# Four state-space scans joined into one stream over chunks of tokens, with GpSimd's arithmetic moved to VectorE

## Chip, core and metric

One NeuronCore of a Trainium2 chip runs the whole block as one program. TensorE (PE in the profile, its weight loads PEld) multiplies matrices, VectorE (DVE) and ScalarE (ACT) work element by element, GpSimd (POOL) too, and SyncE (SP) issues most of the transfers. The metric is the device time of one execution in microseconds; lower is better.

## The reference, cut to what matters

An encoder block on 1040 tokens (16 meta tokens and 1024 of the input) of width 1024: one wide projection, a convolution branch, a bidirectional Mamba-2 branch, a gated merge, and a mixture of 16 experts. The change touches the projections and the Mamba-2 branch.

```python
proj = jnp.einsum('btd,dk->btk', u, w_in[l])          # conf_a, conf_g, z, xbc, dt, gates
xbc = jax.nn.silu(depthwise_conv(xbc, w_ssm_conv[l], b_ssm_conv[l]))       # 7 taps
# xs: 32 heads of 64; Bs, Cs: 4 groups of 128 states
y = bidir_ssd(xs, dt_raw, ssm_dt_bias[l], ssm_a_log[l], Bs, Cs, ssm_d[l])
y = rms_norm(y * jax.nn.silu(z), w_ssm_norm[l])
branch_ssm = jnp.einsum('btc,cd->btd', y, w_ssm_out[l])

# ssd_scan, one direction, chunks of 128 tokens:
y_diag = jnp.einsum('bcgls,bcgjls,bcsgjp->bclgjp', cb, decay, xd)          # within a chunk
states = jnp.einsum('bclgn,bcgjl,bclgjp->bcgjpn', Bc, decay_to_end, xd)
# prev: carry * chunk_decay + states, from chunk to chunk
y_off = jnp.einsum('bclgn,bcgjpn,bcgjl->bclgjp', Cc, prev, jnp.exp(a_cs))  # from the state
# bidir_ssd: forward + backward + d_skip * xs
```

## The kernel before

The kernel is written in Tile: a scheduler lays out every engine's queue ahead of time from the program's order, from marked priorities (`tc.high_priority`) and from its own timeline; on the chip each queue then runs strictly in that order, and an instruction that waits holds all behind it.

The front of the program has two kinds of work. **Projections:** 73 blocks of 128 columns of `w_in`, each in three parts of some 347 tokens (a third). A third is 24 matmuls in fp16 (lines 97 to 99, three products of split operands) into a PSUM tile `mm`, of which there are three. `xbc_tile` (line 362) copies a third from PSUM on ACT and then runs the 7-tap convolution `po` on DVE (line 378); `do_conf` (line 313) makes `ci` and leaves 30 taps (line 335) in a list, from which `some_taps` (line 308) takes a few at a time; `ci` and `co` have one buffer. `gate_tile` (line 340) and `z_tile` (line 350) apply tanh; z's product on DVE (line 358) reads PSUM itself. Weights are converted by ACT (line 224) and DVE (line 225).

**Scans:** `group(g)` (line 531) runs the four groups one after the other. For each of 9 chunks, `within` (line 560) loads the rows of decay, makes them on ACT, multiplies by `cb` on DVE (line 584), and `add_within` (line 589) adds the result `py` to the sum `xs` of the whole group (line 600). `state` and `pass_state` (lines 602 and 617) carry the state forward and backward, two halves for each chunk: `yo` times `er` on DVE (line 628), the sum on GpSimd (line 630), the new state by GpSimd (line 639) and DVE (line 641). `scaled` (line 552) makes `xw` on GpSimd (line 556). The projections of the next group are spread between the halves by `fill`. `turn` (line 387) transposes `po` and stores it to `xk_d`; it is called 4 or 6 thirds after its tile.

A group begins with loads of `Bt`, `Ct` and `xs` for all tokens and ends with all taps that are left, the gating product (line 677) and the store of `yz_d`. GpSimd's queue also holds the stores to DRAM. After the fourth group, `y_group` (line 741) loads `yz_d` and `conf_norm` (line 708) loads `conf_d`, both on ACT's queue, and the next stage multiplies by `w_ssm_out`. The experts (from about 1720 us) are the larger part of the program.

## Time and profile before

| | us |
|---|---|
| median of 3 runs (3063.12 to 3075.85) | 3065.05 |
| the profiled execution | 3077.56 |
| its span, first to last instruction | 3075.9 |
| PE busy in it | 2772.1 (90%) |
| DVE busy | 2214.2 (72%) |
| ACT busy | 1683.7 (55%) |
| POOL busy | 827.2 (27%) |

The profiled execution has 1.7 us around its span and lies 12.5 us above the median. Times in the views are microseconds from the span's start. The program can be cut by its PE work: setup to 85, projections and scans to 1243 (the four groups' first scan products start at 233, 478, 756 and 1009), the branch outputs to 1720, the experts to the end.

### The profile page before, as it was taken

Reading aid. Unit: us, or ns where it says so; the run is one execution under the profiler, and the core shown is the slowest. Engines: PE = TensorE matmul, PEld = TensorE weight load, DVE = VectorE, ACT = ScalarE, POOL = GpSimd, SP = SyncE. Lnnn points to the kernel's source line nnn. Section 1 sums busy time; section 2 is a strip of 40 time slices with the busy share of each in tenths; the row PEclk is TensorE's granted clock in tenths of the full one; section 3 lists DMA queues with packets and bytes.
Section 4 is the critical chain, followed back from the end, with each engine's and each line's share of the span. In section 5 each row is a group of like instructions: output and inputs, shape, how many; then the busy total and the mean of one; then the engine's idle time right before and its main releaser. Section 6 shows DMA issues by size and latency. Waiting matters only on the chain. (4 is left out here: it accounts for less than half of the span.)

```text
span 3075.9 us, 64985 instructions
## 1 busy us (share of the span) xinstructions
PE 2772.1 (90%) x27584; PEld 2372.7 (77%) x27584; DVE 2214.2 (72%) x2747; ACT 1683.7 (55%) x2499; POOL 827.2 (27%) x714
## 2 busy tenths in 40 slices
PE   6789889898999889498999798999999999999996
PEld 4556556565656556498978698999999999999996
DVE  6857966995995798757646587777677777777673
ACT  6646565645665541244313376666666666666643
POOL 1115534542642462223000001112221222222213
PEclk8899999898999989799999899999999999999998
DMA  5345555547456551531533688999999999999994
GB/s 146 116 141 156 161 169 201 163 130 230 154 177 193 185 165 64 184 100 49 184 100 126 244 325 291 333 334 333 327 338 327 318 333 334 325 340 343 341 320 142
DMA packets 370675, 687.88 MB, mean 224 GB/s; under 512 B 31713, under 2 KB 139585, under 8 KB 370377
## 3 DMA queue, kind: packets, MB, share of 16 engines
q1 hardware_dynamic: 335376, 580.64, 55.4%
q0 software_dynamic: 24928, 71.69, 7.7%
q10 hardware_dynamic: 10080, 31.40, 3.3%
q8 instruction: 216, 3.54, 0.5%
q14 instruction: 75, 0.61, 0.1%
HBM read 608.64 MB, written 75.01 MB: 222 GB/s over the span
## 5 line engine op out<-in xcount | busy, mean ns | idle before, releaser
L97 PE MATMUL gu<-xT,wh 128*128 128x130 f16 x3968 | 698.9, 222 | 3.7 <-ACT sil L1134 3.7
L99 PE MATMUL gu<-xT,wl 128*128 128x130 f16 x3968 | 697.7, 220 | 1.2 <-DVE wl L1105 1.1
L98 PE MATMUL gu<-xT,wh 128*128 128x130 f16 x3968 | 698.8, 220 | 0.0
L1091 ACT ACTIVATE junk<-wst 128x2048 bf16<-128x2048 f32 x248 | 473.8, 1910 | 385.4 <-DMA wst<-in_w_exp_gate_dram 321.4
L1105 DVE SCALAR_TENSOR_TENSOR wl<-wst,sc,wh 128x2048 f16<-128x2048 f32 x248 | 572.6, 2346 | 26.9 <-ACT wh L1102 23.9
L98 PEld LDWEIGHTS <-wh 128*128 128x128 f16 x4856 | 480.9, 99 | 82.8 <-issue 38.2
L97 PEld LDWEIGHTS <-wh 128*128 128x128 f16 x4856 | 475.3, 98 | 51.7 <-issue 7.6
L99 PEld LDWEIGHTS <-wl 128*128 128x128 f16 x4832 | 471.3, 98 | 47.5 <-DVE wl L1105 1.5
L1157 PE MATMUL dn<-ac,wst 128*128 128x130 f32 x3840 | 459.3, 277 | 0.0
L1157 PEld LDWEIGHTS dn<-ac,wst 128*128 128x128 f32 x3840 | 440.7, 191 | 0.0
L1176 POOL DMA_INDIRECT h<-yo,idx x60 | 181.9, 3032 | 911.2 <-DVE yo L1175 758.3
L335 DVE SCALAR_TENSOR_TENSOR co<-ci,ct,co 128x1040 f32<-128x1040 f32 x240 | 356.0, 1484 | 3.8 <-ACT co L332 1.7
L97 PE MATMUL mm<-uh,wh 128*128 128x346 f16 (+3 forms) x888 | 280.6, 316 | 22.7 <-DVE st L358 11.2
L97 PE MATMUL mm<-uh,wl 128*128 128x346 f16 (+1 forms) x864 | 275.9, 319 | 17.6 <-DVE st L358 7.9
L98 PE MATMUL mm<-ul,wh 128*128 128x346 f16 (+3 forms) x888 | 280.2, 316 | 0.0
L99 PE MATMUL mm<-uh,wh 128*128 128x346 f16 (+3 forms) x888 | 279.3, 315 | 0.0
L98 PE MATMUL mm<-ul,wl 128*128 128x346 f16 (+1 forms) x864 | 275.3, 319 | 0.0
L99 PE MATMUL mm<-uh,wl 128*128 128x346 f16 (+1 forms) x864 | 275.3, 319 | 0.0
L1102 ACT ACTIVATE wh<-wst,sc 128x2048 f16<-128x2048 f32 x124 | 241.3, 1996 | 19.4 <-DVE sc L1068 17.9
L556 POOL TENSOR_TENSOR xw<-xk,dtw 128x512 f32<-128x512 f32 (+1 forms) x136 | 200.5, 1486 | 129.9 <-DMA xk<-xk_d 82.6
L581 ACT ACTIVATE row<-row,cst 128x128 f32<-128x128 f32 (+1 forms) x576 | 168.9, 378 | 108.0 <-DMA row<-cs_d 106.0
L378 DVE SCALAR_TENSOR_TENSOR po<-pre,sp,po 128x1040 f32<-128x1040 f32 x144 | 204.4, 1420 | 2.7 <-ACT po L375 1.6
(358 smaller groups left out, 4887.9 us busy)
## 6 DMA issues: line engine op xcount, KB each, us to landing
wst<-in_w_exp_gate_dram SPq DMA_DIRECT2D x128, 1024.0 KB, 8.1
wst<-in_w_exp_up_dram SPq DMA_DIRECT2D x128, 1024.0 KB, 9.5
wst<-in_w_exp_down_dram SPq DMA_DIRECT2D x128, 1024.0 KB, 7.9
wr<-in_w_in_dram SPq DMA_DIRECT2D x73, 512.0 KB, 5.3
row<-cs_d SPq DMA_DIRECT2D x64, 512.0 KB, 5.0
xk<-xk_d SPq DMA_DIRECT2D x92, 320.0 KB, 3.6
er<-ecs_d SPq DMA_DIRECT2D x120, 128.0 KB, 3.2
xk_d<-xt POOLq DMA_DIRECT2D x20, 512.0 KB, 4.7
```

What stands on the lines that cost most here:

```text
L97: pe.matmul(ps, wh(k), xh(k), start=(k == 0), stop=False)
L98: pe.matmul(ps, wh(k), xl(k), start=False, stop=False)
L99: pe.matmul(ps, wl(k), xh(k), start=False, stop=(k == K - 1))
L335: dve.scalar_tensor_tensor(co, ci[:, m:m + T], ct[:, m:m + 1], co, op0=OP.mult, op1=OP.add)
L378: dve.scalar_tensor_tensor(po, pre[:, m:m + T], sp[:, j, m:m + 1], po, op0=OP.mult, op1=OP.add)
L556: pool.tensor_mul(heads(o[:L]), heads(xk[:L, :512]), dtw[:L, c, w, hs].unsqueeze(2).to_broadcast([L, HG, 64]))
L581: act.activation(out=E[:L, j, :L], in_=E[:L, j, :L], func=AF.Relu, scale=-1.0, bias=cs)
L1091: act.activation(out=junk, in_=t[m][b], func=AF.Square, accum_out=sq[:, b, m:m + 1])
L1102: act.activation(out=wh[m][0], in_=t[m][0], func=AF.Copy, scale=sc[:, 1, m:m + 1])
L1105: dve.scalar_tensor_tensor(wl[m][b], t[m][b], sc[:, 1, m:m + 1], wh[m][b], op0=OP.mult, op1=OP.subtract)
L1157: pe.matmul(last["dn"][b // 3][:, b % 3], t[:, k, b * P:b * P + P], ac[:, 2 * i + k], start=(i + k == 0 and b % 3 == 0), stop=(i == 7 and ...
L1176: nc.gpsimd.indirect_dma_start(out=h2_d[b], in_=yo[:, h], in_offset=None, compute_op=OP.add, out_offset=bass.IndirectOffsetOnAxis(ap=r.idx ...
```

## The change

- The four groups' scans form one list of 36 chunks and 72 halves; chunks of the next group are prepared while the last ones of a group run. No group waits for its taps to end.
- The sum is kept by chunk: `xa` (ten buffers) is loaded from `xs_d` for one chunk, and `add_to` adds `py` and both directions' `er` on DVE. When a chunk's last term is in, its part of `sz_d` is loaded into a buffer of `er` (of which there are two), multiplied and stored to `yz_d`, which is now one DRAM tile for each group. `Bt` and `Ct` are replaced by chunk loads `bc_` and `Cc`.
- D is put in by ACT when `po` is stored; the gate's factor by ACT in `z_tile` (`zt`), whose product on DVE now reads no PSUM. z and gate are staged by thirds.
- `xw`, the new state's product and the sum go from GpSimd to DVE. GpSimd keeps the stores and the fills.
- `cb` gets a PSUM buffer of its own; `st` keeps one. `po` has three buffers; the convolution has a higher priority; `turn` comes 8 thirds after its tile. Projections are in another order, and the taps taken per half are 2, 4, 3, 5.

```diff
-    sz_d = dram.tile([16, P, T], F32, name="sz_d")
-    yz_d = dram.tile([16, P, T], F32, name="yz_d")
+    sz_d = [dram.tile([4, P, T], F32, name=f"sz_d{g}") for g in range(GR)]
+    yz_d = [dram.tile([4, P, T], F32, name=f"yz_d{g}") for g in range(GR)]
...
         def gate_tile(j):
             w = wtile(OFF_GATE + j * P)
-            st = stage.tile([P, T], F32, name="st")
             for t0, n in NCH:
                 ps = proj(w, t0, n)
+                st = stage.tile([P, 348], F32, name="st")
                 with soon():
-                    act.activation(out=st[:, t0:t0 + n], in_=ps, func=AF.Tanh, scale=w[3])
+                    act.activation(out=st[:, :n], in_=ps, func=AF.Tanh, scale=w[3])
+                nc.gpsimd.dma_start(gate_d[j, :, t0:t0 + n], st[:, :n])
                 yield
-            nc.gpsimd.dma_start(gate_d[j], st)
 
         def z_tile(j):
             w = wtile(OFF_Z + j * P)
-            pool.tensor_copy(zinv[:, j:j + 1], w[3])
-            st = stage.tile([P, T], F32, name="st")
             for t0, n in NCH:
                 ps = proj(w, t0, n)
+                st, zt = [stage.tile([P, 348], F32, name="st") for _ in range(2)]
                 with soon():
-                    act.activation(out=st[:, t0:t0 + n], in_=ps, func=AF.Tanh, scale=w[3])
-                    dve.scalar_tensor_tensor(st[:, t0:t0 + n], st[:, t0:t0 + n], 1.0, ps, op0=OP.add, op1=OP.mult)
+                    act.activation(out=st[:, :n], in_=ps, func=AF.Tanh, scale=w[3])
+                    act.activation(out=zt[:, :n], in_=ps, func=AF.Copy, scale=w[3])
+                dve.scalar_tensor_tensor(st[:, :n], st[:, :n], 1.0, zt[:, :n], op0=OP.add, op1=OP.mult)
+                nc.gpsimd.dma_start(sz_d[j // 4][j % 4, :, t0:t0 + n], st[:, :n])
                 yield
-            nc.gpsimd.dma_start(sz_d[j], st)
+            gated.append(j)
+
+        gated = []
...
-            po = b1.tile([P, T], F32, name="po", bufs=2)
+            po = b1.tile([P, T], F32, name="po", bufs=3)
             act.activation(out=po, in_=pre[:, 0:T], func=AF.Identity, scale=sp[:, j, 0:1], bias=sp[:, j, 7:8])
-            with tc.high_priority(offset=200):
+            with tc.high_priority(offset=900):
                 for m in range(1, TS):
                     dve.scalar_tensor_tensor(po, pre[:, m:m + T], sp[:, j, m:m + 1], po, op0=OP.mult, op1=OP.add)
                 act.activation(out=po, in_=po, func=AF.Silu)
-            nc.gpsimd.dma_start(xs_d[g][i] if i < 4 else bc_d[g][i - 4], po)
+                if i < 4:
+                    act.activation(out=pre[:, 0:T], in_=po, func=AF.Copy, scale=d2[:, 4 * g + i:4 * g + i + 1])
+            nc.gpsimd.dma_start(xs_d[g][i] if i < 4 else bc_d[g][:, i - 4], pre[:, 0:T] if i < 4 else po)
             if i < 5:
-                xt = b1.tile([P, NTT, P], F32, name="xt")
-                later.extend([(third[0] + (6 if g else 4), lambda c0=c0: turn(g, i, po, xt, c0)) for c0 in (0, 1, 5)])
+                later.extend([(third[0] + 8, lambda c0=c0: turn(g, i, po, c0)) for c0 in (0, 1, 5)])
...
+            xt = b1.tile([P, 4, P], F32, name="xt", bufs=2)
             with soon():
-                act.activation(out=xt[:L, c0:c0 + len(cs)], in_=ps[:L, :len(cs)], func=AF.Copy)
-            cols = slice(i * P, i * P + P)
-            if c0 == 0:
-                nc.gpsimd.dma_start(xk_d[g][0, :NMETA, cols], xt[:NMETA, 0])
-            elif c0 == 5:
-                nc.gpsimd.dma_start(xk_d[g][1:, :, cols].rearrange("c p n -> p c n"), xt[:, 1:])
+                act.activation(out=xt[:L, :len(cs)], in_=ps[:L, :len(cs)], func=AF.Copy)
+            nc.gpsimd.dma_start(xk_d[g][c0:c0 + len(cs), :L, i * P:i * P + P].rearrange("c p n -> p c n"),
+                                xt[:L, :len(cs)])
+            if c0 == 5:
+                turned_.add((g, i))
...
+        first = x_(0, 4) + c_(0) + x_(0, 5, 0) + g_(0) + x_(0, 1, 2) + g_(1) + x_(0, 3) + z_(0, 1, 2)
+        plan = [x_(1, 4) + z_(3) + x_(1, 5, 0) + c_(1) + x_(1, 1) + g_(2) + x_(1, 2, 3) + g_(3, 4) + z_(4, 5),
+                x_(2, 4) + z_(6) + c_(2) + z_(7) + x_(2, 5, 0, 1) + g_(5) + x_(2, 2, 3) + c_(3) + z_(8, 9),
+                x_(3, 4) + z_(10) + x_(3, 5) + z_(11) + c_(4) + x_(3, 0, 1) + g_(6) + x_(3, 2, 3) + g_(7, 8) + z_(12, 13),
+                z_(14, 15) + c_(5) + g_(9, 10) + c_(6) + g_(11, 12) + c_(7) + g_(13, 14, 15)]
...
+                def scaled(g, xk, c, w, d):
+                    L = TOK[c][1]
+                    hs = slice(32 * d + HG * g, 32 * d + HG * g + HG)
+                    o = s2.tile([P, 512], F32, name="xw", bufs=3)
+                    dve.tensor_mul(heads(o[:L]), heads(xk[:L, :512]),
+                                   dtw[:L, c, w, hs].unsqueeze(2).to_broadcast([L, HG, 64]))
+                    return o
+
+                sums = {}
+
+                def sum_of(g, c):
+                    t0, L = TOK[c]
+                    if (g, c) not in sums:
+                        xa = s2.tile([P, 4, P], F32, name="xa", bufs=10)
+                        nc.sync.dma_start(xa[:, :, :L], xs_d[g][:, :, t0:t0 + L].rearrange("i p t -> p i t"))
+                        sums[g, c] = [xa, 0]
+                    return sums[g, c]
+
+                def add_to(g, c, y):
+                    t0, L = TOK[c]
+                    s = sums[g, c]
+                    dve.tensor_add(s[0][:, :, :L], s[0][:, :, :L], y[:, :, :L])
+                    s[1] += 1
+                    if s[1] == (2 if c in (0, 8) else 3):
+                        assert all(4 * g + i in gated for i in range(4))
+                        sz = s2.tile([P, 4, P], F32, name="er")
+                        nc.sync.dma_start(sz[:, :, :L], sz_d[g][:, :, t0:t0 + L].rearrange("i p t -> p i t"))
+                        dve.tensor_mul(sz[:, :, :L], sz[:, :, :L], s[0][:, :, :L])
+                        nc.gpsimd.dma_start(yz_d[g][:, :, t0:t0 + L].rearrange("i p t -> p i t"), sz[:, :, :L])
...
+                    bc_ = s2.tile([P, 2, P], F32, name="bc_")
+                    nc.sync.dma_start(bc_[:, :, :L], bc_d[g][:, :, t0:t0 + L])
...
+                    sum_of(g, c)
+                    yield
+                    ps = sps.tile([P, P], F32, name="cb")
+                    pe.matmul(ps[:L, :L], bc_[:, 0, :L], bc_[:, 1, :L], start=True, stop=True)
+                    yield
...
+                    with tc.high_priority(offset=700):
+                        add_to(g, c, py)
...
+                    if c != (8 if d else 0):
+                        sum_of(g, c)
+                        Cc = s2.tile([P, P], F32, name="Cc")
+                        nc.sync.dma_start(Cc[:, :L], bc_d[g][:, 1, t0:t0 + L])
...
-                                    pool.tensor_mul(heads(Sn), heads(S),
-                                                    etot[:, c, hs].unsqueeze(2).to_broadcast([P, HG, 64]))
...
+                                dve.tensor_mul(heads(Sn), heads(S),
+                                               etot[:, c, hs].unsqueeze(2).to_broadcast([P, HG, 64]))
...
+                units = [(g, c) for g in range(GR) for c in range(NTT)]
+                halves = [(g, d, 8 - i if d else i) for g in range(GR) for i in range(NTT) for d in range(2)]
+                work = thirds([i for p_ in plan for i in p_])
...
-                        some_taps(4 if g in (1, 3) else 2)
...
-                    some_taps(TK)
-                    for i in range(4):
-                        sz = b1.tile([P, T + 6], F32, name="pre", bufs=2)[:, :T]
-                        nc.sync.dma_start(sz, sz_d[4 * g + i])
-                        dve.scalar_tensor_tensor(sz, sz, zinv[:, 4 * g + i:4 * g + i + 1], xs[:, i], op0=OP.mult,
-                                                 op1=OP.mult)
-                        nc.gpsimd.dma_start(yz_d[4 * g + i], sz)
...
+                    if m == per - 3:
+                        while later:
+                            later.pop(0)[1]()
+                    some_taps((2, 4, 3, 5)[g])
...
```

Where the instructions stand now, at three places. First DVE's queue in the middle of the third group's scan. `xs` and `xa` are sums, `S` the state, `po` and `co` the two convolutions. Before:

```order
L600 TENSOR_TENSOR xs<-xs,py 128x4x128
L335 SCALAR_TENSOR_TENSOR co<-ci,ct,co 128x1040
L584 TENSOR_TENSOR row<-row,cbm_7606 128x1024
L584 TENSOR_TENSOR row<-row,cbm_7608 128x1024
L628 TENSOR_TENSOR er<-yo,er 128x512
L641 TENSOR_TENSOR S_7695<-st,S_7695 128x512
L378 SCALAR_TENSOR_TENSOR po<-pre,sp,po 128x1040
```

Now:

```order
L562 TENSOR_TENSOR xa<-xa,py 128x512
L545 TENSOR_TENSOR xw<-xk,dtw 128x512
L207 TENSOR_SCALAR sc<-sc 128x3
L380 SCALAR_TENSOR_TENSOR po<-pre,sp,po 128x1040
L562 TENSOR_TENSOR xa<-xa,er 128x512
L648 TENSOR_TENSOR er<-yo,er 128x512
L658 TENSOR_TENSOR S_8231<-S_7989,etot 128x512
```

The products `xw` and `S` by `etot` and the sum `xa` by `er` stand between DVE's own work; before, they were on GpSimd's queue.

Second SP's queue, late in a group's scan (the last group before, the second now). `er` takes turns between two buffers. Before:

```order
L613 DMA er_10555<-ecs_d_74 64x512 x2
L549 DMA xk_10800<-xk_d3_72 128x640
L195 DMA wr_10467<-in_w_in_dram 128x8x128
L613 DMA er_10648<-ecs_d_74 64x512 x2
L613 DMA er_10804<-ecs_d_74 64x512 x2
```

Now:

```order
L629 DMA Cc_6777<-bc_d1_62 128x16
L578 DMA bc__7429<-bc_d2_63 128x2x128
L633 DMA er_6330<-ecs_d_80 64x512 x2
L567 DMA er_6409<-sz_d1_68 128x4x128
L633 DMA er_6458<-ecs_d_80 64x512
L567 DMA er_6578<-sz_d1_68 128x4x128
```

Every second buffer of `er` now holds a chunk of `sz_d`, and loads of the next group's chunks stand between them.

Third ACT's queue at the end of the front, where the last tanh (`st`) is followed by the next stage's loads. Before:

```order
L766 DMA gt<-gate_d 128x1040 x2
L346 ACTIVATE st<-mm,sc 128x346 x2
L160 ACTIVATE wh<-wr 128x512
L712 DMA cc<-conf_d 128x1040 x7
L748 DMA yst<-yz_d 128x1040 x2
L712 DMA cc<-conf_d 128x1040
L750 ACTIVATE yh<-yst,cp 128x1040 x2
```

Now:

```order
L345 ACTIVATE st<-mm,sc 128x346 x2
L160 ACTIVATE wh<-wr 128x512
L774 DMA yst<-yz_d_71 128x1040 x2
L776 ACTIVATE yh<-yst,cp 128x1040 x2
L778 ACTIVATE yst<-yst 128x1040 x2
L774 DMA yst<-yz_d_71 128x1040 x2
L776 ACTIVATE yh<-yst,cp 128x1040 x2
L778 ACTIVATE yst<-yst 128x1040
L738 DMA cc<-conf_d 128x1040
```

The loads of `yz_d` have gone ahead of those of `conf_d`.

## Rows read from the trace of the kernel before

**Rows 1.** Windows: each engine's busy time by stage of the front; then the totals.

```profile
core 0: us, PE busy (x) PEld busy (x) DVE busy (x) ACT busy (x) POOL busy (x), PEclk, DMA share, GB/s
85.00:233.00 148.00, 124.13 (x795) 81.53 (x795) 102.20 (x116) 79.10 (x152) 23.67 (x47) 0.92 0.43 132
233.00:478.00 245.00, 214.14 (x1525) 146.42 (x1524) 190.99 (x207) 142.83 (x285) 114.79 (x106) 0.95 0.54 172
478.00:756.00 278.00, 241.81 (x1675) 162.65 (x1673) 229.35 (x246) 151.27 (x296) 109.88 (x109) 0.93 0.56 175
756.00:1009.00 253.00, 228.81 (x1613) 154.63 (x1613) 190.18 (x213) 149.29 (x296) 115.36 (x111) 0.95 0.57 181
1009.00:1243.00 234.00, 212.32 (x1501) 145.00 (x1502) 207.80 (x215) 93.23 (x197) 107.61 (x80) 0.95 0.41 130
85.00:1243.00 1158.00, 1021.22 (x7102) 690.23 (x7103) 920.51 (x997) 615.72 (x1224) 471.31 (x450) 0.94 0.51 161
1243.00:1300.00 57.00, 19.26 (x93) 17.11 (x90) 35.60 (x26) 18.32 (x25) 15.82 (x11) 0.72 0.61 210
```

**Rows 2.** Waits of PE, 85 to 1243: total us, times, longest.

```profile
PE mm L392 <- ACT po L379: 34.5, 8, 12.5
PE mm L97 <- DVE st L358: 19.1, 12, 3.3
PE st L570 <- DVE S L641: 15.6, 8, 4.1
PE st L633 <- issue: 9.4, 4, 3.9
PE py L596 <- POOL xw L556: 7.8, 4, 2.7
```

**Rows 3.** Groups by form, 85 to 1243: count, busy us, mean ns, idle before.

```profile
L335 DVE SCALAR_TENSOR_TENSOR co<-ci,ct,co 128x1040 f32<-128x1040 f32 x237 | 352.1, 1486 | 3.8 <-ACT co L332 1.7
L378 DVE SCALAR_TENSOR_TENSOR po<-pre,sp,po 128x1040 f32<-128x1040 f32 x139 | 197.9, 1425 | 2.7 <-ACT po L375 1.6
L584 DVE TENSOR_TENSOR row<-row,cbm 128x1024 f32<-128x1024 f32 x64 | 106.8, 1696 | 4.7 <-ACT row L582 4.7
...
L556 POOL TENSOR_TENSOR xw<-xk,dtw 128x512 f32<-128x512 f32 x124 | 188.4, 1530 | 108.7 <-DMA xk<-xk_d 61.5 <-PE st L633 30.9 <-PE py L596 8.6
L630 POOL TENSOR_TENSOR xs<-xs,er 128x512 f32<-128x512 f32 x60 | 97.6, 1628 | 76.2 <-DVE er L628 76.0
L639 POOL TENSOR_TENSOR S<-S,etot 128x512 f32<-128x512 f32 x56 | 90.0, 1609 | 36.4 <-ACT S L637 19.0 <-DVE S L641 17.3
```

**Rows 4.** Timeline of DVE and of POOL, 1200 to 1207: start, duration, instruction.

```profile
1203.64 2.08 DVE L335 SCALAR_TENSOR_TENSOR co<-ci,ct,co 128x1040 f32<-128x1040 f32 x1
1205.64 0.68 DVE L600 TENSOR_TENSOR xs<-xs,py 128x512 f32<-128x512 f32 x1
1206.23 1.29 DVE L335 SCALAR_TENSOR_TENSOR co<-ci,ct,co 128x1040 f32<-128x1040 f32 x1
...
1200.64 3.98 POOL L556 TENSOR_TENSOR xw<-xk,dtw 128x512 f32<-128x512 f32 x2
```

**Rows 5.** Line 901: a DVE product of two SBUF tiles, GpSimd at rest; min/median/max ns.

```profile
L901 DVE TENSOR_TENSOR hn<-xt,wffn x18: 669/688/693, 1622.5 to 1714.6; 128x512 f32<-128x512 f32 x16, 16x512 f32<-16x512 f32 x2
```

**Rows 6.** Wait of SP's queue, and DMA issues with median us to landing, 85 to 1243.

```profile
SPq L613 <- POOL xs L630: 232.4, 51, 11.2
...
er<-ecs_d SPq DMA_DIRECT2D x120, 128.0 KB, 3.2
...
yz_d<-pre POOLq DMA_DIRECT2D x12, 520.0 KB, 6.8
```

**Rows 7.** PE's wait after 1243, and ACT's timeline there.

```profile
PE mm L97 <- ACT yh L750: 31.0, 2, 28.9
...
1243.95 15.94 ACTq L712 DMA_DIRECT2D cc<-conf_d  x6
...
1271.05 1.16 ACT L750 ACTIVATE yh<-yst,cp 128x1040 fp32r<-128x1040 f32 x1 [26.61 <-DMA yst<-yz_d]
```

265 lines of the change are left out of this document (120 added, 145 removed).

## The prediction

> **What bounds the kernel now.** I read the windows first, since the page's shares are means over stages that have little in common. Only the front, 85 to 1243 us, and the 57 us behind it are touched; the experts' instructions keep their order, so I leave everything from 1300 us on as it is. In the front PE is busy 1021.2 of 1158 us at a mean granted clock of 0.94, and DVE 920.5 us, that is 79% [rows 1]. Neither is full over the whole stage, yet they come close together: in the last group DVE holds 208 of 234 us (89%), in the first only 191 of 245. So the front is bound by PE and DVE in turn, and the waits tell by what. PE's idle time there is 137 us. Its largest parts are transposes that wait for the convolution (34.5), projections whose PSUM tile waits for z's product on DVE (19.1), the product `cb` that waits for the PSUM buffer it shares with the state (15.6), and 17.2 around `xw` from GpSimd: 7.8 named so and 9.4 before the state's product, which reads `xw` too, put down to "issue" [rows 2]. After a wait PE also runs for a while at the lower of its two levels, 1.2 GHz: a mean of 0.94 is 12% of the stage, some 139 us, at half speed.
>
> At 1243 the last projection is done and PE waits 28.9 us for `yh`. ACT's queue shows why: seven loads of `conf_d` stand ahead of the first of `yz_d` and hold the queue 15.9 us, and `yh` runs at 1271 after an idle time of 26.6 [rows 7]. In these 57 us PE is busy 19 at clock 0.72 [rows 1].
>
> **The change part by part.** All differences are made on the profiled execution, 3077.56 us, and then taken from the median, 3065.05, 12.5 us lower.
>
> DVE takes on 136 products `xw` (124 and 12 short ones), 60 sums and 56 state products, 252 in all. The nearest row is a product of two SBUF tiles of the same size with GpSimd at rest, 0.688 us [rows 5]: 252 x 0.688 = 173 us. From below: these overlap at their ends as two taps do (0.07 us), so 155. The gating products by chunk cost what the four long ones of each group did, the sums with `py` stay, and z's product changes only its operand.
>
> What DVE gets back is the time that GpSimd takes from it. A tap that starts at 1203.64, beside two `xw` products, takes 2.08 us, the next one 1.29; the sum between them, which reads PSUM, takes 0.68 as ever [rows 4]. Over the stage a tap has a mean of 1.486 and a convolution step 1.425, against 1.29: 237 x 0.196 + 139 x 0.135 = 65 us. The products of line 584 have a mean of 1.696 against at most twice 0.688: 64 x 0.32 = 20 [rows 3, 5]. Together 85; conversions read two tiles as well and are not counted. The Trainium skill's page "SBUF — State Buffer", section "Who interferes with whom", says that a DVE instruction with two SBUF inputs and a GpSimd instruction that reads SBUF exclude one another, and that the loser waits for the whole instruction. Row and rule agree on which instructions suffer, but by the rule each meeting would cost up to a whole `xw`, 1.53 us, and 240 of them 367 us on one engine or the other; I keep the 85 that the means show on DVE.
>
> So DVE goes from 920 to about 1008 us (920 - 85 + 173), or 990 by the lower bound, beside PE's 1021. ACT gains 48 copies `zt` of a third of a tile; a copy of a whole one takes 1.16 us [rows 7], so they cost between 19 and 56 us on an engine that is busy 616 of 1158 [rows 1], near the lower end by size. I take nothing for them: ACT's other work hides them, unless a row of decay that it waits for holds its queue, and then PE waits for the PSUM tile behind it, at most those 56. GpSimd loses 376 us of arithmetic; its stores become more and smaller, but behind no product.
>
> PE's waits: `turn` comes later and behind a convolution of higher priority, z's PSUM tile is freed by ACT, `cb` has its own buffer, `xw` no longer queues behind GpSimd. That can take away 34.5 + 19.1 + 15.6 + 17.2 = 86 us and with it part of the 139 us at half speed. It does so only if DVE keeps up. A bound from the better side: all 137 us of idle time go. From the other: DVE's share cannot rise above the 0.89 of its fullest stretch, 1008 / 0.89 = 1133, a gain of 25. I take DVE at 91%, since groups no longer end with a flush of taps and contention is gone: 1008 / 0.91 = 1108, a gain of **50 us**.
>
> The tail: the loads of `yz_d` now come first on ACT, and three of its four DRAM tiles are full long before. What is late next is DVE. The last convolution's 30 taps start when nine thirds of gates are left: 30 x 1.29 = 39 us, with a conversion, two splits and two `yl` among them some 5 more by their sizes, against 216 matmuls at 1021.2 / 7102 = 0.144 us, 31 us. The third and fourth `yl` stand behind all taps, so PE still stops for about 15 us and then runs a few at half speed. Now the 57 us hold work worth 19.3 x 0.72 = 14 at the full clock; 43 are lost. I put the loss after at 14 to 20 and the gain at **28 us**. `conf_norm` shifts behind more matmuls of the next stage, which hides it unless DVE is late there.
>
> Sum: 50 + 28 = 78 us, 3065 - 78 = **2987 us**.
>
> **The rivals.** *The ring of `er` stops DVE (slower).* In the second half of each group every chunk that is complete needs an `er` buffer for `sz_d`, and the next one can be loaded only when the store to `yz_d` has landed: 3.2 (load, as `er`) + 0.7 + up to 6.8 (store, of a tile twice as large) = 10.7 us [rows 5, 6], where a half lasts (1243 - 233) / 72 = 14.0. SP's queue is strict, and it already stood 232 us for `er` buffers. DVE's queue is strict too: behind `er` stand the taps, the weights' conversions and the state, hence PE. It decides from the point where a round takes more than a half. With SP's mean wait of 232.4 / 51 = 4.6 us on top a round takes 15.3, 1.3 over; with the longest, 11.2, it is 7.9 over. At 3.5, 9 halves in 4 groups are 126 us, against the 78 gained: 3065 + 48 = 3113. For it speaks that two loads and a store now share what one load had; against it, that the sum which frees `er` takes DVE 0.7 us where GpSimd took 1.63 [rows 3]. Chance 0.17.
>
> *DVE is the wall.* It stays at 0.87 of the stage, 1008 / 0.87 = 1159: all that PE's waits gave back returns as waits for DVE, and only the tail is left, 3065 - 28 = 3037. The second group speaks for it: DVE 229 and PE 242 of 278 us, neither above 0.87 [rows 1]. Chance 0.22. The Trainium skill's page "Perfetto Trace Analysis", section "Optimizing Scalar/DVE Operations", says that work may be moved off a saturated DVE, to GpSimd even, and this change does the reverse; the page adds that a move between these two may not help because they share a port, and rows 4 bear out that part.
>
> *PE's waits all go.* The 86 us and 24 of the time at half speed leave, the tail gives 38: 3065 - 148 = 2917. It needs DVE at 1008 / 1048 = 96%. Chance 0.15.
>
> *Nothing comes of it.* The tail's gain is paid back in the next stage and the front stays. Within 0.5%. Chance 0.08.
>
> **How the numbers follow.** The forecast has the remaining 0.38. A measurement can tell about 0.5%, 15 us, from no change. Faster: 0.38 + 0.22 + 0.15 = 0.75; same 0.08; slower 0.17. The range takes in the wall, the full gain and most of the slower case: 2905 to 3100, with about 0.05 below and 0.12 above. The forecast's own range is 2950 to 3020.
>
> **What would show it.** Taps at 1.29 to 1.33 us throughout; DVE busy 980 to 1010 us before the last projection, at about 91%; no wait of PE for `po`, for z's `st` or for the state's buffer above a few us; the last projection near 1193; PE's stop behind it near 15 us, ended by `yl`. If the ring decides, DVE's `er` lines show idle time ended by DMAs from `ecs_d` and `sz_d`, in the second half of each group. If DVE is the wall, it is above 85% with PE waiting on its lines. I am wrong altogether if PE waits on ACT, whose queue I cost at nothing, or on something in the experts, whose order is the same.

## The result, and the profile after

| us | before | after |
|---|---|---|
| median of the runs | 3066.48 | 3033.77 |
| profiled execution, its span | 3077.56, 3075.9 | 3033.02, 3031.3 |
| first scan of groups 2, 3, 4 | 478, 756, 1009 | 454, 723, 967 |
| last projection done | 1243.3 | 1221.7 |
| first product of the branch (`yh`) | 1272.3 | 1226.6 |
| its 301st product | 1338.9 | 1286.7 |
| its last product | 1584.8 | 1542.7 |
| first product of the experts | 1738.2 | 1695.9 |

The changed kernel is 1.2% faster: ratio 0.9884, 95% interval 0.9859 to 0.991, some 33 us where 78 were forecast. The two profiled executions differ by 44.5, because that of before lies 11 us above its median. Every ratio below is against the kernel before, run beside it on the same chip; what a run gains on the changed kernel is the difference of the two ratios, times 3066 us, and not that of two medians. The marks in the table are starts and ends of single matmuls in the two traces, and they say where the time went. Up to the last group's first scan 42 us were gained, and the last group lost 20.6 of them. (It also has 39 matmuls more than before, 1540 against 1501, some 6 us that moved there from ahead of it; 36 and 15 would be the figures without them.) Behind the last projection 30.6 were gained up to the 301st product of the branch, and 10 of these were gone by its last product.

The windows of the changed kernel by group, then the whole front and the stretch behind it (they answer to [rows 1]; columns as there):

```profile
core 0: us, PE busy (x) PEld busy (x) DVE busy (x) ACT busy (x) POOL busy (x), PEclk, DMA share, GB/s
233.00:454.00 221.00, 200.27 (x1445) 135.95 (x1445) 185.43 (x259) 144.31 (x287) 26.55 (x53) 0.95 0.63 186
454.00:723.00 269.00, 232.21 (x1649) 156.27 (x1648) 221.71 (x311) 159.34 (x311) 34.03 (x68) 0.93 0.64 187
723.00:967.00 244.00, 221.75 (x1602) 151.99 (x1600) 218.46 (x298) 155.03 (x307) 32.76 (x64) 0.94 0.63 187
967.00:1221.50 254.50, 217.83 (x1540) 147.06 (x1538) 212.36 (x275) 94.63 (x202) 25.33 (x45) 0.93 0.49 144
85.00:1221.50 1136.50, 1005.72 (x7104) 680.36 (x7101) 946.26 (x1271) 644.92 (x1276) 145.43 (x287) 0.94 0.58 171
1221.50:1260.00 38.50, 28.15 (x142) 26.66 (x141) 30.55 (x24) 17.68 (x26) 12.63 (x6) 0.82 0.65 224
```

DVE is busy 946 of 1136.5 us, 83%; the forecast had 1008 at 91%. In the last group PE is busy 217.8 us instead of 212.3, at a granted clock of 0.93, but the group takes 254.5 instead of 234.

PE's waits in the front, 85 to 1221.5 us (total, times, longest), which answer to [rows 2]:

```profile
PE mm L395 <- ACT po L381: 26.1, 6, 7.5
PE mm L97 <- DVE ci L326: 17.3, 2, 16.4
PE mm L97 <- ACT xt L399: 15.9, 7, 6.1
PE cb L587 <- DVE cbm L592: 14.3, 5, 5.8
PE mm L97 <- ACT pre L374: 11.1, 5, 5.9
PE st L652 <- DVE S L660: 10.2, 9, 2.2
PE mm L395 <- ACT st L356: 8.5, 2, 5.1
...
PE py L614 <- DVE row L602: 5.4, 1, 5.4
```

The wait for `xw` from GpSimd (7.8) is gone (5.4 us of waits for it now stand on DVE), and so is that for z's product (19.1). The wait for `po` is down from 34.5 to 26.1. In their places stand waits for `ci` and `cbm` (`cb` behind its mask) on DVE and for `xt` and `pre` on ACT. PE's idle time is 131 us of 1136.5 (1136.5 - 1005.7), where it was 137 of 1158.

DVE's groups by form in the front (mean ns of one behind the busy time), against [rows 3, 5]:

```profile
L334 DVE SCALAR_TENSOR_TENSOR co<-ci,ct,co 128x1040 f32<-128x1040 f32 x232 | 300.3, 1295 | 2.6 <-ACT co L331 0.3
L380 DVE SCALAR_TENSOR_TENSOR po<-pre,sp,po 128x1040 f32<-128x1040 f32 x139 | 179.0, 1293 | 6.0 <-ACT po L377 5.7
L545 DVE TENSOR_TENSOR xw<-xk,dtw 128x512 f32<-128x512 f32 x124 | 84.3, 681 | 4.6 <-PE py L614 2.0 <-DMA xk<-xk_d 1.6 <-PE st L652 1.0
L602 DVE TENSOR_TENSOR row<-row,cbm 128x1024 f32<-128x1024 f32 x64 | 76.3, 1216 | 23.1 <-ACT row L600 23.1
```

Taps and convolution steps are at 1.295 and 1.293 us, and the 1024-wide product at 1.216 instead of 1.696. The added products cost 0.681. Nothing of GpSimd's interference is left in these rows.

### The profile page after: what moved, and what is told of

Same layout as the page of the kernel before. It is cut to its first block, busy times and chain, and to the rows that moved or that the text cites. A ratio compares the mean times of both kernels' runs of the same rounds, so it can differ in the third digit from the quotient of the medians.

```text
span 3031.3 us, 65413 instructions
## 1 busy us (share of the span) xinstructions
PE 2757.7 (91%) x27584; PEld 2364.2 (78%) x27584; DVE 2245.9 (74%) x3023; ACT 1714.3 (57%) x2551; POOL 501.3 (17%) x546
## 5 line engine op out<-in xcount | busy, mean ns | idle before, releaser
L97 PEld LDWEIGHTS <-wh 128*128 128x128 f16 x4856 | 475.6, 98 | 57.6 <-issue 12.5
L334 DVE SCALAR_TENSOR_TENSOR co<-ci,ct,co 128x1040 f32<-128x1040 f32 x240 | 314.9, 1312 | 2.8 <-ACT co L331 0.3
L97 PE MATMUL mm<-uh,wl 128*128 128x346 f16 (+1 forms) x864 | 271.6, 314 | 18.2 <-ACT pre L374 9.6
L99 PE MATMUL mm<-uh,wl 128*128 128x346 f16 (+1 forms) x864 | 270.9, 314 | 0.0
L1128 ACT ACTIVATE wh<-wst,sc 128x2048 f16<-128x2048 f32 x124 | 241.3, 1996 | 17.3 <-DVE sc L1094 16.6
L380 DVE SCALAR_TENSOR_TENSOR po<-pre,sp,po 128x1040 f32<-128x1040 f32 x144 | 185.5, 1293 | 6.0 <-ACT po L377 5.7
L97 PE MATMUL mm<-yh,wh 128*128 128x346 f32 (+1 forms) x480 | 158.9, 338 | 25.1 <-DVE acc L802 14.9
```

The costliest lines, as they stand in the source:

```text
L97: pe.matmul(ps, wh(k), xh(k), start=(k == 0), stop=False)
L99: pe.matmul(ps, wl(k), xh(k), start=False, stop=(k == K - 1))
L334: dve.scalar_tensor_tensor(co, ci[:, m:m + T], ct[:, m:m + 1], co, op0=OP.mult, op1=OP.add)
L380: dve.scalar_tensor_tensor(po, pre[:, m:m + T], sp[:, j, m:m + 1], po, op0=OP.mult, op1=OP.add)
L1128: act.activation(out=wh[m][0], in_=t[m][0], func=AF.Copy, scale=sc[:, 1, m:m + 1])
```

## Why the last group lost: one buffer of `ci`

The largest single wait of the changed front is this. DVE's timeline ahead of it, then PE's first row behind it:

```profile
1159.21 12.00 DVE L334 SCALAR_TENSOR_TENSOR co<-ci,ct,co 128x1040 f32<-128x1040 f32 x9
...
1178.17 3.97 DVE L334 SCALAR_TENSOR_TENSOR co<-ci,ct,co 128x1040 f32<-128x1040 f32 x3
...
1182.80 0.94 DVE L326 SCALAR_TENSOR_TENSOR ci<-sg,mm 128x348 f32<-128x348 f32 x2
```

```profile
1183.36 0.45 PE L97 MATMUL mm<-uh,wh 128*128 128x346 f16 x1 [16.39 <-DVE ci L326]
```

PE is about to write the next PSUM tile of conf 7's projection; the tile is free once DVE has formed `ci` from the one before. `ci` has one buffer, and all 30 taps of conf 6 read it. DVE is not idle: it has taps in its queue from 1159 to 1182 and forms `ci` only then, two pieces at once. PE stands for 16.39 us. The same stretch as windows:

```profile
1150.00:1167.00 17.00, 16.98 (x121) 11.88 (x119) 16.75 (x19) 1.10 (x2) 0.00 (x0) 1.00 0.01 3
1167.00:1183.40 16.40, 0.04 (x1) 0.03 (x1) 15.23 (x19) 0.00 (x0) 2.45 (x6) 0.56 0.25 66
1183.40:1189.40 6.00, 6.00 (x22) 3.12 (x22) 0.34 (x1) 0.55 (x1) 1.50 (x2) 0.50 0.83 273
1189.40:1220.00 30.60, 30.60 (x210) 20.35 (x209) 28.58 (x24) 7.21 (x11) 4.35 (x8) 1.00 0.18 59
```

The granted clock is down to 0.50, the 1.2 GHz level, for 20.5 us from 1168.9, but 14.5 of these lie in the stop itself. PE works at the low level for 6 us and so loses 3 there.

**e1: a second buffer of `ci`.**

```
-            ci = cfp.tile([P, T + 30], F32, name="ci")
+            ci = cfp.tile([P, T + 30], F32, name="ci", bufs=2)
```

> The changed kernel with a second buffer for `ci`, the tile that the 31 taps of a conf column read; all else as in the changed kernel. In its trace VectorE's `ci` product of the last conf column waits for the 30 taps of the conf column before, TensorE stops 16.4 us for it at 1167.0 us, and the 20.5 us behind that run at half the clock (some 10 us lost). Theory A (the last group is held by this chain, not by VectorE's amount of work): the stop goes, the last projection ends 15 to 27 us earlier (1195 to 1206 instead of 1221.5), and the whole takes 3005 to 3020 instead of 3034 us. Rival B (VectorE's work is the wall in the last group, 212 busy of 254.5 us, so that what is taken out of the stop comes back as waits for `yo`, `cb` or `st`, or the taps that are put off make the branch wait): last projection not before 1215, whole 3028 or more. Front, up to 967 us: the same within 4 us in both.

Ratio 0.9793 (0.9773 to 0.9813), median 3006.6: 28 us less than the changed kernel, by one buffer. The last group as a window:

```profile
966.90:1175.50 208.60, 206.00 (x1541) 140.79 (x1540) 174.57 (x243) 92.90 (x201) 19.39 (x35) 1.00 0.54 160
```

The last projection ends at 1175.5, 46 us earlier; PE needs 206.0 us at clock 1.00, and its idle time falls from 36.7 to 2.6. That is more than the stop and the 3 us behind it: the small waits for `py`, `xw` and `S` in this group went too, since DVE did 38 us less there and put taps off to a time behind the projections (its last tap ends at 1263 instead of 1240.5). By the branch's last product 27 of the 46 us are left. My "some 10 us" for the half clock in the expectation was too much. Behind the projections PE stands 17.55 us for `yh` (ACT and DVE split each column of `yz_d` into two parts, `yh` and `yl`, which PE multiplies). ACT's timeline says why:

```profile
1190.71 1.25 ACT L331 ACTIVATE co<-ci,cp,ct 128x1040 f32<-128x1040 f32 x1 [14.04 <-DMA conf_d<-co]
...
1191.87 2.20 ACT L776 ACTIVATE yh<-yst,cp 128x1040 fp32r<-128x1040 f32 x2
```

The first tap of conf 7, on ACT, waits for `co`, the tile the taps gather in, which has one buffer as well and must first be stored. `yh` stands behind it.

**e6: the same buffers, the conf columns further apart.**

```
-                 z_(14, 15) + c_(5) + g_(9, 10) + c_(6) + g_(11, 12) + c_(7) + g_(13, 14, 15)]
+                 c_(5) + z_(14, 15) + g_(9) + c_(6) + g_(10, 11, 12) + c_(7) + g_(13, 14, 15)]
```

> The changed kernel with the last group's tiles in another order, the conf columns further apart: conf 5, z 14, z 15, gate 9, conf 6, gate 10 to 12, conf 7, gate 13 to 15 (in the changed kernel two gate tiles stand between conf 6 and conf 7, 6 thirds of some 3.5 us for 39 us of taps; now three tiles). One buffer of `ci` as before. Theory A (the stop of 16.4 us is the 39 us of taps that do not fit between two conf columns): the stop falls to 5 us or less, the last projection ends 8 to 25 us before 1221.7, whole 3010 to 3026. Rival B (VectorE has fallen behind for other reasons and the taps would be late at any place): the stop stays over 10 us or comes back as waits for `yo`, `py` or `yh`, whole 3028 to 3040.

Ratio 0.981 (0.9786 to 0.9835), median 3019.6. The stop is gone, the last projection ends at 1198.2, 23.5 us earlier, and 23 us show in the ratio. DVE is busy 943 us in this front, 946 in that of the changed kernel, so hardly any work was put off here. So the stop was a matter of spacing: between conf 6 and conf 7 the changed plan has two gate tiles, 6 thirds of about 3.5 us, for 39 us of taps. Three tiles were enough here.

**e13: the second `ci` in the kernel before.** The edit is that of e1.

> The kernel before with a second buffer for `ci`, nothing else. In the trace of before no wait of TensorE for `ci` stands in the last group, with three to four tiles between two conf columns. Theory A (the chain of conf columns is the bound of the last group only since the change drew them together and gave VectorE GpSimd's work): last group's length (234 us from its first scan to the last projection) within 8 us, whole 3056 to 3076. Rival B (the chain held the last group before already, hidden in other waits): last group shorter by 12 us or more, whole under 3052.

Ratio 1.001 (0.9995 to 1.0025): nothing, and its last group takes 232 us, as before (234). In the trace of the kernel before, PE waits 0.2 us for `ci` in the whole front. The chain was there before, but had room; the change took the room away.

**e5, e9, e10: two buffers of `co` too.** The first of these has `ci` as in e1 and takes the memory from cbm0, cbm1 and `ct`, the tile of the taps' factors, which get one buffer each.

```
-            co = cfp.tile([P, T], F32, name="co")
-            ct = cfp.tile([P, TK], F32, name="ct", bufs=2)
+            co = cfp.tile([P, T], F32, name="co", bufs=2)
+            ct = cfp.tile([P, TK], F32, name="ct", bufs=1)
```

> The changed kernel with two buffers for `ci` and for `co`, the tile in which the taps gather (to make room, cbm0, cbm1 and ct in one buffer each). With two of `ci` alone the last projection ended at 1175.5 instead of 1221.7 us, but TensorE then stood 17.55 us for `yh`, because ScalarE's queue stood 14.0 us at the first tap of the last column, which waited for `co` to be stored. Theory A (a chain of buffers): that stop falls under 6 us, the last projection ends within 1170 to 1182, the first branch product starts before 1187, and the whole takes 2988 to 3001 us. Rival B (by now VectorE has the work to do, 60 taps of 1.3 us left at the end of the projections, and what does not wait for `co` waits for VectorE's `yl` and the norm of conf): first branch product before 1190, but 6 to 12 us given back in the branch, whole 3001 to 3012.

Ratio 0.9769 (0.9742 to 0.9795), 3005.1. PE still stood 16.6 us for `yh`. I had made the next link myself, as ACT's timeline shows:

```profile
1182.90 1.25 ACT L331 ACTIVATE co<-ci,cp,ct 128x1040 f32<-128x1040 f32 x1 [8.60 <-DVE ct L330]
```

In e9 the factors are scaled in place in `cp`, so that there is no `ct` to wait for (`ci`, `co` and the two cbm as in e5):

```
-            dve.tensor_scalar_mul(ct, cp[:, j, 0:TK], wa[2])
+            ct = cp[:, j, 0:TK]
+            with soon():
+                dve.tensor_scalar_mul(ct, ct, wa[2])
```

> The changed kernel with two buffers for `ci` and for `co` once more, but the taps' factors scaled in place in `cp` instead of in the tile `ct`, which stood in one buffer in the run before with two of both: there ScalarE waited 8.6 us for `ct` on VectorE, which waited for the taps of the column before, and TensorE 16.6 us for `yh` at 1173.1. Theory A (that stop was the chain through `ct`, put there by making room): it falls to 6 us or less, first branch product before 1186, whole 2985 to 3000 us. Rival B (the last sums of the stream, their gate products and the stores to yz_d end only at 1183, so `yh` waits for them whatever ScalarE does): the stop stays at 10 to 18 us, now ended by the DMA of yz_d or by the gate product, whole 2998 to 3010.

Ratio 0.9799 (0.9782 to 0.9816): no better than e1. The stop at `yh` fell to 5.3 us, but PE then stood 12.5 at `yl`, and 9.9 at a later `yh`. That is neither of the two that I had named. (The profiled execution took 3023.3 us, the longest of the six, so its marks may lie later than they mostly do.) DVE's timeline there:

```profile
1197.46 4.93 DVE L335 SCALAR_TENSOR_TENSOR co<-ci,cp,co 128x1040 f32<-128x1040 f32 x4
1202.31 1.29 DVE L778 SCALAR_TENSOR_TENSOR yl<-yst,cp,yh 128x1040 fp32r<-128x1040 f32 x1
```

Now the taps are DVE's backlog, and `yl` stands behind four of them. e10, which has e9's buffers and e6's spacing:

> The run with two buffers of `ci` and `co` and the factors in place, and the conf columns of the last group further apart (conf 5, z 14, z 15, gate 9, conf 6, gate 10 to 12, conf 7, gate 13 to 15). Theory A (with two buffers the spacing has nothing left to do): within 6 us of the run with two buffers. Rival B (spacing spreads VectorE's taps and so frees the end of the group): 6 to 15 us less than with two buffers alone.

Ratio 0.9791 (0.9771 to 0.9812), the same as e9 within its interval; PE stood 13.4 us for `yl`. With the chain of buffers open, it is in these two runs DVE's queue at the end of the front that PE waits for.

## The other suspects in the front

**e7: a ring of its own for the gate's tile.** This tests the rival that the shared ring of `er`, the two buffers that both loads take turns in, stops DVE. DVE's idle time for the two loads of that ring in the changed kernel:

```profile
DVE er L568 <- DMA er<-sz_d: 27.7, 19, 4.6
...
DVE er L648 <- DMA er<-ecs_d: 14.8, 8, 3.5
```

```
-                        sz = s2.tile([P, 4, P], F32, name="er")
+                        sz = s2.tile([P, 4, P], F32, name="sz")
```

> The changed kernel with a ring of its own, two buffers, for the gate's tile `sz`, which shares the two buffers of `er` (the states' decay rows) in the changed kernel. Tests the rival that a shared ring stops VectorE: in the changed kernel VectorE is idle 27.7 us (19 times) for sz and 14.8 us (8 times) for er's rows between 85 and 1221.5 us. Theory A (TensorE does not wait for these products, so the ring costs little): those waits fall by half or more, TensorE's waits stay within 10 us of what they were, whole 3026 to 3042. Rival B (the ring is where the front's missing gain went): last group's first scan 10 us or more before 966.8, whole 3000 to 3022.

The same waits with the ring apart:

```profile
DVE sz L568 <- DMA sz<-sz_d: 5.5, 3, 2.5
...
DVE er L648 <- DMA er<-ecs_d: 3.6, 1, 3.6
```

They fall from 42.5 to 9.1 us. Ratio 0.9847 (0.9821 to 0.9872), median 3030.9; the intervals of e7 and of the changed kernel just overlap, and the difference is about 11 us. The last projection ends 11 us earlier as well, 5 of them by the last group's first scan. So the ring costs about 11 us by both, though the ratios alone don't tell it clear of noise; the 126 of the rival it does not cost. The expectation's total for theory A held, though not its "costs little" to the letter.

**e2: the decay rows one chunk earlier.** ACT's longest wait in the front is for these rows, and the silus and copies that PE waits for stand behind them (the edit also leaves cbm0 and cbm1 one buffer each, to make room). The changed kernel:

```profile
ACT row L599 <- DMA row<-cs_d: 112.7, 32, 10.2
...
ACT pre L374 <- DMA xs_d<-pre: 21.6, 6, 9.2
```

```
+                        n = units.index(unit)
+                        for u in units[n:n + 2]:
+                            if u not in rows_of and (u != unit or n == 0):
+                                load_rows(*u)
...
-                        row = s2.tile([P, HG, P], F32, name="row", bufs=4)
+                        row = s2.tile([P, HG, P], F32, name="row", bufs=6)
```

> The changed kernel with the decay rows (`row`, DMA from cs_d) asked for one chunk of tokens earlier, in six buffers instead of four (cbm0 and cbm1 in one buffer each to make room). In the changed kernel ScalarE's queue stands 112.7 us in 32 waits for these rows between 85 and 1221.5, up to 10.2 us each, and the silus, xt copies and pre copies for which TensorE waits are queued behind. Theory A (ScalarE's queue held by late rows is where the front's missing gain went): the row waits fall under 30 us, TensorE's waits for po, xt and pre (26, 16 and 19 us) fall by half or more, the last group's first scan comes 12 to 30 us before 967, and the whole takes 3005 to 3022 us. Rival B (TensorE waits on ScalarE because ScalarE has its work from VectorE and the DMA just then, and the rows were only the place where the wait shows): the row waits fall, but po, xt and pre move by under 10 us together, and the whole is 3026 to 3040.

The same wait in e2:

```profile
ACT row L605 <- DMA row<-cs_d: 93.8, 26, 10.8
```

Ratio 0.993 (0.9905 to 0.9956), 3047.2, if anything slower than the changed kernel; the last projection ends at 1221.8, where it was. But the wait fell only to 93.8 us: the scheduler, which orders each engine's instructions, moved ACT's work on the rows forward with the loads (its first step now stands 64 us ahead of the chunk's first product `py`, median of the 36 chunks, instead of 39). So this run doesn't decide whether late rows hold ACT. That stays open.

**e8: a tile of its own for tokens times D.** In the changed kernel this copy goes back into `pre`, and ACT waits 21.6 us for its store.

```
+                    pd = b1.tile([P, T], F32, name="pd", bufs=1)
-                    act.activation(out=pre[:, 0:T], in_=po, func=AF.Copy, scale=d2[...])
+                    act.activation(out=pd, in_=po, func=AF.Copy, scale=d2[...])
...
+            nc.gpsimd.dma_start(xs_d[g][i] if i < 4 else bc_d[g][:, i - 4], pd if i < 4 else po)
```

> The changed kernel with a tile of its own for the tokens times D, which the changed kernel writes back into `pre`, whose two buffers are then held until the store to xs_d has landed. In the changed kernel ScalarE stands 21.6 us (6 times, up to 9.2) for that store, and TensorE 21.5 us in all for pre copies. Theory A (this new wait is part of what the front did not gain): ScalarE's wait for xs_d goes, TensorE's waits for pre fall by 10 us or more, last projection 6 to 20 us before 1221.7, whole 3014 to 3028. Rival B (the last group's chain ends the front anyway and swallows what is gained ahead of it): last group's first scan earlier by 5 to 20 us, last projection within 5 us of 1221.7, whole 3028 to 3038. Rival C: nothing at either place.

Ratio 0.9882 (0.9859 to 0.9906): nothing that can be measured. ACT's wait is gone, the last group's first scan comes at 956.6 instead of 966.8, and the last projection at 1214.3, 7 us earlier. The stop for `ci` is still 16.2 us. This lies between A and B in the trace and shows nothing in the time.

**e12: without the 48 copies `zt`.** The gate's product then lacks a factor for each channel, which this kernel leaves out.

```
-                st, zt = [stage.tile([P, 348], F32, name="st") for _ in range(2)]
+                st = stage.tile([P, 348], F32, name="st")
...
-                    act.activation(out=zt[:, :n], in_=ps, func=AF.Copy, scale=w[3])
-                dve.scalar_tensor_tensor(st[:, :n], st[:, :n], 1.0, zt[:, :n], op0=OP.add, op1=OP.mult)
+                dve.scalar_tensor_tensor(st[:, :n], st[:, :n], 1.0, ps, op0=OP.add, op1=OP.mult)
```

> The changed kernel without the copy `zt`: VectorE takes the gate's product from PSUM as the kernel before did, and the factor of the column's scaling is left out altogether (so the gate's product lacks a factor for each channel). ScalarE is rid of 48 copies (some 0.55 us each, 26 us) and PSUM of nothing. Tests the step of the prediction that costed these copies at nothing unless ScalarE's queue was held. Theory A (they cost little): whole 3026 to 3042, TensorE's wait for VectorE's `st` back at 10 to 20 us. Rival B (ScalarE's queue is where the front is held, so that 26 us less there show): last group's first scan 10 us or more before 966.8, whole 3005 to 3024.

Ratio 0.9911 (0.9893 to 0.9929), 3043.9: the copies cost nothing. The 25 us less on ACT brought no gain, and the last projection ends at 1224.3. PE's wait for z's `st` did not come back either (2.3 us in all), which I had expected at 10 to 20; so what ended that wait was not the copy alone, and which part did I did not test.

**e3 and e4: GpSimd's arithmetic by itself.** e3 is the changed kernel with the three operations given back to GpSimd, e4 the kernel before with them on DVE.

```
-                    dve.tensor_mul(heads(o[:L]), heads(xk[:L, :512]),
+                    pool.tensor_mul(heads(o[:L]), heads(xk[:L, :512]),
...
```

> The changed kernel with the arithmetic given back to GpSimd: the scaled tokens `xw`, the state's decay product `S` and the sums `xa` of the states' outputs run on GpSimd as in the kernel before; the stream over the groups, the stages of D and the gate, the loads and the tail are those of the changed kernel. Between 85 and 1221.5 us this takes about 250 operations of 0.68 us (170 us) off VectorE, and brings back what taps lost beside GpSimd's products (taps 1.42 to 1.49 instead of 1.295 us, in all 85 by the prediction, 126 by comparison of the two traces). Theory A (the move is worth little beside the rest, since VectorE is not the bound at 83%): VectorE busy 870 to 920, whole 3025 to 3050, TensorE's wait for GpSimd's `xw` back at 15 us or so. Rival B (the move from GpSimd is what gains): whole 3060 or more. Rival C (the move costs, the stream gains all of it): under 3020.

> The kernel before with one part of the change alone: the three GpSimd operations (scaled tokens, decay product, sum of the states' outputs) on VectorE, all else as before. Theory A (the contention is as large as the two traces say, 126 us, so VectorE's work grows by only some 45 us and its queue feeds TensorE sooner): taps 1.29 to 1.31 us, VectorE busy 950 to 980 of the front, TensorE's wait for `xw` from GpSimd gone, whole 3045 to 3066. Rival B (VectorE becomes the bound in the single groups, with their serial ends): whole 3075 to 3110. Rival C (no effect): 3060 to 3072, with TensorE's waits changing place only.

e3: ratio 0.9939 (0.9919 to 0.9959), 17 us more than the changed kernel. e4: 0.9972 (0.9956 to 0.9987), some 9 us less than before. The medians, 3052.5 and 3064.4, settle little between the expectations: the first lies just above the range of its A, the second in those of A and C. DVE's first two groups by form in the front, e3 and then e4:

```profile
L334 DVE SCALAR_TENSOR_TENSOR co<-ci,ct,co 128x1040 f32<-128x1040 f32 x228 | 340.6, 1494 | 2.9 <-ACT co L331 0.5
L380 DVE SCALAR_TENSOR_TENSOR po<-pre,sp,po 128x1040 f32<-128x1040 f32 x139 | 208.3, 1504 | 1.5 <-ACT po L377 1.1
```

```profile
L335 DVE SCALAR_TENSOR_TENSOR co<-ci,ct,co 128x1040 f32<-128x1040 f32 x224 | 290.1, 1295 | 2.1 <-ACT co L332 0.3
L378 DVE SCALAR_TENSOR_TENSOR po<-pre,sp,po 128x1040 f32<-128x1040 f32 x139 | 179.5, 1294 | 2.2 <-ACT po L375 1.1
```

The same taps take 1.494 us with GpSimd at work and 1.295 without, in either kernel. So the move is worth 9 us alone and 17 in the changed kernel; what is left of the gain, about 19 us, is the stream, the projections' factors and the tail.

**e14: the tail.** In the kernel before, `conf_d`'s loads stood on ACT's queue ahead of those of `yz_d` [rows 7]. Here SP's queue has them:

```
-            nc.scalar.dma_start(cc[j], conf_d[j])
+            nc.sync.dma_start(cc[j], conf_d[j])
```

> The kernel before with the eight loads of conf_d issued on SP's queue instead of ScalarE's, so that they no longer stand ahead of the loads of yz_d there; all projections and scans stand in the order of before. In the trace of before ScalarE's queue was held 15.94 us by six of them and TensorE stood 28.9 us for `yh` at 1243.3. Theory A (the tail's stop is the order of these loads on ScalarE's queue, so the changed kernel's gain there is not from gating by chunks): stop of 4 to 9 us, first branch product before 1254, whole 3040 to 3056. Rival B (the gate's products at the group's end and their stores make `yh` late in any case): stop of 18 us or more, whole 3058 to 3072.

Ratio 1.0018 (1.0004 to 1.0033): no gain, and the stop is still 26.4 us. GpSimd's timeline (last sum of the states, last store of the gate's product), then ACT's:

```profile
1237.08 1.29 POOL L630 TENSOR_TENSOR xs<-xs,er 128x64 f32<-128x64 f32 x1 [4.83 <-DVE er L628]
...
1252.15 0.53 POOL L679 DMA_DIRECT2D yz_d<-pre  x1 [1.14 <-DVE pre L677]
```

```profile
1257.76 2.86 ACTq L748 DMA_DIRECT2D yst<-yz_d  x2
1264.34 1.16 ACT L750 ACTIVATE yh<-yst,cp 128x1040 fp32r<-128x1040 f32 x1 [24.05 <-DMA yst<-yz_d]
```

The sum ends at 1238, the gate's products come after it, two at a time because `pre` has two buffers, the last is stored at 1252, and only then can `yz_d`, one DRAM tile in this kernel, be loaded. ACT's held queue hid this. The gate by chunks is not needed to take the stop away: e4 gates whole columns at the end of a group too, with the loads of `yz_d` first on ACT's queue, and its first `yh` has waited only 3 us:

```profile
1258.56 1.16 ACT L750 ACTIVATE yh<-yst,cp 128x1040 fp32r<-128x1040 f32 x1 [3.07 <-DMA yst<-yz_d]
```

There the last store to `yz_d` stands at 1181 us, 73 ahead of the end of the last projection, and PE stops 5.4 us; in the changed kernel it stands at 1184, 38 ahead. So the stop goes with how late the last scan ends against the last projection. Which part of the change makes it end early (the sums on DVE, the stream, the order of the projections) was not taken apart.

**e11: what helped, together.** Two buffers of `ci`, one of `co`, the ring apart, the factors in place, the spacing of e6, one buffer each for cbm0 and cbm1.

```
+            ci = cfp.tile([P, T + 30], F32, name="ci", bufs=2)
...
+            ct = cp[:, j, 0:TK]
...
+                        sz = s2.tile([P, 4, P], F32, name="sz")
...
+                        m = s2.tile([P, P], F32, name=f"cbm{d}", bufs=1)
...
+                 c_(5) + z_(14, 15) + g_(9) + c_(6) + g_(10, 11, 12) + c_(7) + g_(13, 14, 15)]
```

> Two buffers for `ci`, one for `co`, the gate's tile `sz` in a ring of its own, factors in place, conf columns of the last group further apart. By the ratios so far (two of `ci` -28, ring of its own -11, apart -23 us against the changed kernel's 3034, the first and the last against the same stop) the parts sum to 2990 to 2998 if ring and stop are independent (theory A). Rival B (the ring's gain was the same stop in the last group, 10.6 instead of 16.4 us there): 3000 to 3010.

Ratio 0.9746 (0.9728 to 0.9765), median 2994.7 where the kernel before had 3070.5: 42 us less than the changed kernel and faster than both. Front and last group as windows, then PE's waits at their end:

```profile
85.00:1164.90 1079.90, 986.89 (x7104) 671.24 (x7102) 917.80 (x1250) 644.51 (x1276) 143.68 (x283) 0.96 0.59 179
957.40:1164.90 207.50, 205.54 (x1543) 141.02 (x1542) 182.91 (x253) 94.40 (x202) 21.93 (x39) 1.00 0.54 165
```

```profile
PE mm L97 <- ACT yh L777: 7.3, 2, 5.3
PE mm L98 <- DVE yl L778: 3.7, 2, 2.2
```

e1's 28 and e7's 11 make 39, so the sum fits a ring and a chain that are separate losses. It doesn't show it: no run has these two edits alone, and the spacing and the factors in place changed with them. Why PE waits so much less for `yl` here than in e10 (3.7 us, not 13.4) was not taken apart; the two differ in `co` and in the ring.

## Why the prediction missed, step by step

**DVE's work: right in price, too high in sum.** The products cost 0.681 us, and 0.688 was taken. What GpSimd had cost was larger than 85 us: 232 x 0.191 for the taps, 139 x 0.132 for the steps, 64 x 0.480 for the 1024-wide product, and 8 for the conversions, which I had left out: 101. The bound "at most twice 0.688" for the wide product was the loose one; it takes 1.216. The small steps of the weights' scaling (lines 200 to 213 before) went from 47 to 26 us as well; most of the rest of the way from 1008 to 946 is that more instructions overlap at their ends, since the groups' times sum to 48 us more than before and the engine's busy time grew by 26. The lower bound of 155 rests on a wrong reading: two taps in a row don't overlap by 0.07 us, three of them take 3.97. The Trainium skill's page "SBUF — State Buffer", section "Who interferes with whom", agrees on who suffers. Beside the tap of [rows 4] stand, in the same trace, the two wide products ahead of it on DVE and a product `xw` of GpSimd that met none:

```profile
1199.67 4.04 DVE L584 TENSOR_TENSOR row<-row,cbm 128x1024 f32<-128x1024 f32 x2
```

```profile
1195.21 1.21 POOL L556 TENSOR_TENSOR xw<-xk,dtw 128x512 f32<-128x512 f32 x1 [12.55 <-PE st L633]
```

The two wide products and the tap lose 0.8 us each there, 2.4 together, the time of two `xw` alone; so where the engines meet, DVE loses about what the other engine's product takes alone, as the prediction read the rule. The mean of 0.2 us for a tap mixes taps that met GpSimd with those that didn't (the median tap took 1.302 us). The 367 us of the prediction were too many because they let every one of GpSimd's 240 products and sums meet such an instruction. No view counts how many did.

**The front's gain of 50: this step failed.** I took DVE at 91% "since groups no longer end with a flush of taps", and divided. Measured are 21.6, the last projection at 1221.7 and not near 1193. Up to the last group it was 42, 6 of them moved work, not far from the step's size. In the last one the flush is still there: conf 7 flushes conf 6's taps ahead of its own `ci`, and no share of a stage shows that. With a second `ci` the front gives 67.8 instead of 50, with DVE still at 83%, though some 37 us of its work were put off to behind the front. With the spacing alone (e6) it gives 45.1, with nearly all of DVE's work still in it, at 85%. So it was this chain and not DVE's total that held the gain. What would have shown it was in the diff: the thirds between two conf columns of the plan, against 30 x 1.29 us.

**ACT at nothing: held for the copies** (e12). But the sign that I had named for being wrong is there: in the front PE waits 76 us for ACT, 66 before, and 55 for DVE, 53 before. Whether rows of decay hold ACT's queue, the condition I put to it, is open (e2): the projections' waits for `xt` and `pre` rose from 7.4 and 3.2 to 15.9 and 11.1 us, and no run took them away.

**The tail's 28: right in size, not in its end.** The gain by the 301st product is 52.2 - 21.6 = 30.6. PE's stops for `yh` and `yl` behind the last projection:

```profile
PE mm L97 <- ACT yh L776: 8.8, 2, 4.9
PE mm L98 <- DVE yl L777: 1.5, 2, 1.3
```

They sum to 10 us, not 15, and `yh` ends most of it. I had read ACT's held queue as the cause in the kernel before; e14 shows that the gate's last products and stores hold `yh` without it. Then 10 us were given back at the place where I had written that the norm of conf is hidden "unless DVE is late there". DVE's timeline:

```profile
1289.72 13.78 DVE L746 TENSOR_TENSOR cc<-cc,mean 128x1040 f32<-128x1040 f32 x8
1303.43 0.93 DVE L802 TENSOR_TENSOR acc<-mm,acc 128x346 f32<-128x346 f32 x2
```

Eight subtractions of the norm's mean, 13.78 us, stand ahead of the sum that frees PE's PSUM tile, and PE stops 6.5 us there and runs at the 1.2 GHz level behind it. That is read from the trace; no run moved the subtractions.

**The sum.** Of the 47 us between 2987 and 3033.8, 28 are the front, 10 the norm's, less 3 more in the tail and less 2 or 3 in the experts; the other 13 come from the base. I made all differences on an execution 12.5 us above the median, but took them from the median; where in that execution the 12.5 us lie, no trace shows. The median of three runs may be part of it: in 63 later runs, on four chips, the kernel before had medians of 3070.5 to 3074.1.

**The rivals.** The time came out at that of *DVE is the wall*, 3037, by chance and not for its reason: DVE was at 83%, PE's waits were for ACT more than for DVE, the front gained 21.6 us where that rival has none, and one buffer moved its end by 46 us. Something like it shows only behind e1, at the end of the front (12.5 and 13.4 us at `yl` in e9 and e10, but 3.7 in e11). *The ring* exists and costs about 11 us. *PE's waits all go* did not come, since 131 us of idle time are left. *Nothing comes of it* is wrong too: only 10 us of the tail's gain were paid back.

## What to carry to other kernels

A share of busy time can't price a plan: for every tile with one buffer, hold the work that must drain it against the time until the plan writes it again, and do so again wherever the plan was changed. When a chain opens, look for the next link (`co`, then `ct`, then the engine's backlog), and mind that making room by taking a buffer elsewhere can forge one. A queue that is held just ahead of a late instruction needn't be its cause; follow the data back before pricing it.
